# A hybrid decoder trunk on one core: the first product starts with the queries, squares come last, and second halves use a second PSUM pool

## The chip, the core and the metric

The kernel runs on one core of a Trainium2 chip. A core has a matrix engine (TensorE, PE in the rows), a vector engine (VectorE, DVE), a scalar engine for activations and copies (ScalarE, ACT), a general one (GpSimd, POOL), and queues that start transfers from memory; here the queue of SyncE (SP) loads weights, and POOL's queue loads caches and stores results. The metric is the device time of one run in microseconds (us).

## The reference, cut to what matters

Two layers act on 512 prompt tokens and 32 sample tokens (8 sequences of 4), 544 columns in all, of width 1024. Every sub-layer begins with an RMS norm.

```
h = rmsnorm(x, g)                       # x * rsqrt(mean(x*x) + eps) * g
# layer 0: gated linear attention, 4 heads
q, k, v, r, gz = split(h @ w_in)        # 512, 512, 1024, 1024, 16 columns
glog = log_sigmoid(gz @ w_g2 + b_g) / 16
o, state = gla_scan(q, k, v, glog, state)
x = x + (rmsnorm(o, g_norm) * silu(r)) @ w_out
# layer 1: dilated window attention, 3 groups of 16 heads, keys and values of the samples from caches
x = x + combine(groups) @ w_out
# after each layer: convolutional feed-forward, d_ff = 2816
u = h @ w_up
c = causal_conv3(u)
x = x + (silu(gate(c)) * val(c)) @ w_down
```

## The kernel before, in words

Activations lie transposed: the 1024 features are eight tiles (k = 0 to 7) of 128 partitions by 544 tokens. TensorE works on 32-bit numbers that are split in two: `xh` is the rounded high part of x times the norm's gain, `xl` the rest; a weight has `whi` and `wlo`. One product of a 128-column weight block adds `xh*whi`, `xl*whi` and `xh*wlo` over all k. It does so for one half of the tokens and then for the other (two halves of 272, `EVEN`, or 256 and 288, `BYTOK`), so it has 2 x 8 x 3 = 48 matmuls. `product` takes its PSUM tile `ps` from the pool `pm`, which has three buffers. The other pool, `pa`, has five and serves sums of squares (`pss`), gates (`pg`), attention and decoding.

`Normed.add` makes `xh` (ACT) and `xl` (DVE) of an x tile and its square. In the prologue the odd tiles' squares and their sum lie on POOL (`sqp`), the even ones' on ACT and DVE (`sq`, `acc`); elsewhere all squares are ACT's and all sums DVE's. The reciprocal root `rstd` is made when it is first wanted: matmuls with `ones` sum over partitions, ACT takes a logarithm of each half (L181) and an exponential (L124). The norm's factor per token is not in `xh` and `xl`; it is multiplied in where a product is evicted (`scaled`), so an eviction needs `rstd`, the matmuls don't.

The prologue of `gla` loads the gains and the gate weights `wgz`, fills two weight tiles with zeros and puts three copies of the gate weights' high and low parts into them (96 columns each), loads the eight x tiles, and forms the gate product `gz` (48 matmuls), whose eviction needs `rstd`. Then come, for each head, the products q, k and two value products v. For head 0 I call the latter `v0` and `v1`. `gates` and `chain` of a head run as generators between the matmuls of later products (`tick`), and a scheduler then fixes the order on each engine.

In layer 1, four decoding steps j serve the sample tokens, four heads each. `decode_scores` reads keys, `decode_values` the values in seven parts of 1 MB (`vc`, two buffers shared with the keys' `kc`); the matmuls are `pdo`. The out-projection follows; six of its blocks have a last piece, `late`, which adds to x and then feeds the next norm. `ffn` has 22 rounds with two up-products each, evicted with `rstd` into `u` (L566), and down-products that add to x (L196).

Of the kernel before, what the change touches and what calls it, by code (L numbers as in the profile page):

```python
# [11 lines left out]
F32 = mybir.dt.float32  # L12
# [24 lines left out]
def trunk(ctx: ExitStack, tc: tile.TileContext, A, O, stage=4):  # L37
# [58 lines left out]

    def product(w, xh, xl, ranges, done, m=P):

        kt = len(w)
        for n, (a, b) in enumerate(ranges):  # L100
            ps = pm.tile([P, 512], F32, name="ps", tag="ps")
            for k, (hi, lo) in enumerate(w):
                for s, (ww, xx) in enumerate(((hi, xh), (hi, xl), (lo, xh))):
                    mm(ps[:m, :b - a], ww, xx[k][:, a:b],  # L104
                       start=(k == 0 and s == 0), stop=(k == kt - 1 and s == 2))
                if k % 3 == 2 and k < kt - 1:
                    tick()
            done(n, ps[:m, :b - a], slice(a, b))
            tick()


    ident = cp.tile([P, P], F32, name="ident")
    gains = const("gains", [P, 4, KT])
    eps = cp.tile([P, 1], F32, name="eps")
# [5 lines left out]

    last_silu, last_exp = [None], [None]

# [8 lines left out]
    @contextmanager  # L131
    def log_exp():

        with ExitStack() as es:
            if last_silu[0] is not None:
                es.enter_context(tc.issue_after(last_silu[0].ins))
            pre = nc.scalar.preload_act_table_set(LNEXP)
        with tc.issue_after(pre.ins):
            yield
# [4 lines left out]
    class Normed:  # L144
# [3 lines left out]
        def __init__(self, gi):  # L148
            self.gi, self.row, self.acc = gi, None, {}
            self.xh, self.xl = [None] * KT, [None] * KT  # L150

        def add(self, k, x, spare=None):

            g = gains[:, self.gi, k:k + 1]
            h = self.xh[k] = xp.tile([P, NT], F32R, name=f"xh{k}")
            l = self.xl[k] = xp.tile([P, NT], F32R, name=f"xl{k}")
            act(h, x, AF.Copy, scale=g)  # L157
            stt(l, x, g, h.bitcast(F32), ALU.mult, ALU.subtract)  # L158
            i = spare is not None and k % 2
            first = i not in self.acc  # L160
            if i:
                sq = spare.tile([P, NT], F32, name=f"sqp{min(k, 3)}", bufs=2 - first)
                nc.gpsimd.tensor_tensor(out=sq, in0=x, in1=x, op=ALU.mult)
            else:
                sq = xp.tile([P, NT], F32, name="acc" if first else "sq")
                act(sq, x, AF.Square)
            if first:
                self.acc[i] = sq
            else:
                (nc.gpsimd if i else nc.vector).tensor_tensor(out=self.acc[i], in0=self.acc[i], in1=sq, op=ALU.add)  # L170

        @property
        def rstd(self):
            if self.row is None:
                self.row = xp.tile([P, NT], F32, name="rstd")
                with log_exp():
                    for c in (slice(*r) for r in EVEN):
                        ps = pa.tile([P, 512], F32, name="pss", tag="pa")
                        for i, acc in self.acc.items():
                            mm(ps[:, :HN], ones, acc[:, c], start=(i == 0), stop=(i == len(self.acc) - 1))  # L180
                        act(self.row[:, c], ps[:, :HN], AF.Ln, bias=eps, scale=1.0 / 1024)  # L181
                exp(self.row, self.row, scale=-0.5)
            return self.row
# [16 lines left out]
    def gla(nxt):  # L200
# [7 lines left out]

        wz = gconst("wgz", [P, KT, 16])
        whi, wlo = [wp.tile([P, KT, 96], F32R, name=n, tag=n) for n in ("whi", "wlo")]  # L210
        h3, l3 = [t.rearrange("p k (c n) -> p k c n", c=3)[:, :, :, :16] for t in (whi, wlo)]
        wz = wz.unsqueeze(2).to_broadcast([P, KT, 3, 16])
        for t in (whi, wlo):
            nc.vector.tensor_copy(t.rearrange("p k n -> p (k n)"), zero.to_broadcast([P, KT * 96]))
        nc.scalar.copy(h3, wz)
        tt(out=l3, in0=wz, in1=h3.bitcast(F32), op=ALU.subtract)
        nx = Normed(0)
        for k in range(KT):
            x = xtile()
            dma(x, A["xT"][:, k, :])  # L220
            nx.add(k, x, tmp)
        wg2 = gconst("wg2", [96, 512])
        bg = gconst("bg", [P, 4])
        first = load_w(A["wg"][0], KT, 256, "wqk")

        gz = gc.tile([96, NT], F32, name="gz")
        gz3 = gc.tile([96, NT], F32R, name="gz3")
        wg3 = gc.tile([96, 512], F32R, name="wg3")
        product([(whi[:, k], wlo[:, k]) for k in range(KT)], nx.xh, nx.xl, EVEN, scaled(nx, gz, m=96), 96)
        nc.scalar.copy(wg3, wg2)  # L230
# [239 lines left out]
        for h in range(4):  # L470
            G = []
            lanes[1].append(gates(h, G))
            raw = load_w(A["wg"][2 * h], KT, 256, "wqk") if h else first
            q = tmp.tile([P, NT], F32, name="q", bufs=2)
            k = tmp.tile([P, NT], F32, name="k", bufs=2)
            product(split_w(raw, 0, KT, 0), nx.xh, nx.xl, EVEN, scaled(nx, q, P ** -0.5))
            product(split_w(raw, 0, KT, P), nx.xh, nx.xl, EVEN, scaled(nx, k))
            raw = load_w(A["wg"][2 * h + 1], KT, 256, "wv")
            v = [tmp.tile([P, NT], F32, name="vf", bufs=2) for s in range(2)]
            for s in range(2):  # L480
                product(split_w(raw, 0, KT, s * P), nx.xh, nx.xl, EVEN, scaled(nx, v[s]))
            drain()
            lanes[0].append(chain(h, q, k, v, G))
# [8 lines left out]
        for c in range(4):  # L492
            raw = load_w(A["wg"][8 + c], KT, 256, "wr")
            for s in range(2):
# [38 lines left out]
    def ffn(l, x, nx, dst, tables=None, nxt=None):  # L533
        first = load_w(A["wu"][l, 0], KT, 256, "wu")
        with ExitStack() as es:
# [14 lines left out]
            for hf in range(2):  # L550
                gh, gl = [], []
                for ii in range(half):
# [4 lines left out]
                    for s in range(2):  # L557
# [12 lines left out]

                        product(split_w(raw, 0, KT, s * P), nx.xh, nx.xl, BYTOK, done)
                        nc.gpsimd.tensor_copy(  # L572
# [19 lines left out]
                for m in range(KT):  # L592
                    raw = load_w(A["wd"][l, hf, m], half, P, "wd")
                    w = split_w(raw, 0, 6, 0) + split_w(raw, 6, half, 0)
                    product(w, gh, gl, EVEN, added(x[m], x[m]))
                    if hf == 1:
                        (dma if l and m == KT - 1 else dma2)(dst[:, m, :], x[m])
                        if nxt is not None:
                            nxt.add(m, x[m])
# [38 lines left out]
    def dilated(nx, xold, tables, nxt):  # L638
        first = load_w(A["wdi"][0], KT, 256, "wdi")
        with ExitStack() as es:  # L640
# [273 lines left out]
            def decode_scores(j, ks, pace, D):  # L914
# [19 lines left out]
                for part, (cols, width) in enumerate(((((1, 0, 512),), 512), (((0, 0, 128), (2, 128, 384)), 480))):  # L934
# [9 lines left out]
                    for b in range(4):  # L944
# [7 lines left out]
                        if len(kc) < 8:  # L952
                            load()
                    if part:
                        while (2 * j + 1, 1, 0) not in done:
# [9 lines left out]
                done.add(("decode", j))  # L965

            def decode_values(j, vs, pace, D):
                Sd, mx = D["Sd"], D["mx"]
                vc = []

                def load():
                    vc.append(at.tile([P, 4, 512], F32, name="vc", tag="kc"))
                    dma2(vc[-1].rearrange("p a b -> p (a b)"), A["dv"][j, len(vc) - 1])

                load()
                load()
                stt(mx[:, 2:3], mx[:, 0:1], mx[:, 1:2], mx[:, 0:1], ALU.max, ALU.max)
# [29 lines left out]
                for t in range(7):  # L1007
                    for qd in range(4):
                        mm(po[32 * qd:32 * qd + 32, :], PT[:, t, 32 * qd:32 * qd + 32], vc[t][:, qd, :],
                           start=False, stop=(t == 6), skip_group_check=True)  # L1010
                    if t < 5:
                        load()
                    for _ in range(2 * pace if t in (1, 3, 5) else 1 if t == 6 else 0):
                        yield
# [15 lines left out]
            for jj in range(KT):  # L1030
# [59 lines left out]
                if i:  # L1090
                    lanes[1].append(decode_values(j, vs, 9 if j < 3 else 2, D))
                    upto((jj, 1, 0))
# [41 lines left out]
            for m in (6, 0, 1, 2, 3, 4, 5, 7):  # L1134
                if m < 6:
                    product(late[m], ogh[6:], ogl[6:], EVEN, added(x[m], x[m]))
                else:
                    product(split_w(raw, 0, 6, m % 2 * P) + late[m], ogh, ogl, EVEN, old(m))
                nxt.add(m, x[m])
# [76 lines left out]
def layout(inp):  # L1216
# [16 lines left out]
    ch += [w[:, 2048 + 256 * c:2048 + 256 * (c + 1)] for c in range(4)]  # L1233
    d["wg"] = np.stack([chunk(c) for c in ch])
    d["wgz"] = chunk(w[:, 3072:]).reshape(P, KT, 16)
    wg2 = np.zeros((96, 512), np.float32)
    for r in (0, 32, 64):
        wg2[r:r + 16] = a["gla_w_gate2"][0]
# [95 lines left out]
```

## Time and profile before

| | us |
|---|---|
| median of three runs | 1783.75 |
| range | 1783.56 to 1787.02 |
| the profiled execution | 1782.73 |
| its span in the trace | 1781.0 |
| TensorE busy | 1762.5 (99%) |
| DVE, ACT, POOL busy | 1088.0, 802.6, 225.4 |

The span is the stretch of the trace from its first to its last record; the execution's own time is 1.7 us more. A busy TensorE may still run at half of its clock: the granted clock is a column of its own, 1.00 being 2.4 GHz and 0.50 being 1.2 GHz. Times in the trace count from the start of the span. In a timeline the number behind the start is how long the instruction, or the merged run of them, took until its end; matmuls overlap, so their spacing is read from their starts.

### The profile page before, as it was taken

What the parts mean: (1) busy time and instruction counts of PE and PEld (TensorE: products, weight loads), DVE (VectorE), ACT (ScalarE), POOL (GpSimd) and SP (SyncE); (2) the same over time, 40 slices, a digit from 0 to 9 for tenths busy, and PEclk for the clock granted to TensorE, in tenths of its full rate; (3) what the DMA queues carried; (4) which work ended last, traced back from release to release, by engine and by line L of the source; (5) the groups of instructions that cost most, each with busy time, mean ns of one, the idle gap of its engine ahead of it and who ended that gap; (6) DMA issues with size and microseconds to landing.
All of it is one profiled execution on the core that took longest, in us unless ns stands there. A gap on an engine that the chain in (4) does not pass through costs nothing. (4 is left out here: it accounts for less than half of the span.)

```text
span 1781.0 us, 35680 instructions
## 1 busy us (share of the span) xinstructions
PE 1762.5 (99%) x14774; PEld 1672.8 (94%) x14774; DVE 1088.0 (61%) x2552; ACT 802.6 (45%) x1549; POOL 225.4 (13%) x416
## 2 busy tenths in 40 slices
PE   7999999999999999999999999999999999999999
PEld 7999999999999999988998889889888999999999
DVE  7665656764467645666575657666665666347652
ACT  5554544442244435645556465537454434224331
POOL 3000101110011110111012010211121111002100
PEclk9999999999999999999999999999999999999999
DMA  5034432432422244346436643654473222222222
GB/s 183 27 136 152 139 120 74 154 105 82 138 92 95 82 139 180 105 168 220 172 118 208 226 150 129 218 180 151 168 253 139 95 77 75 92 101 96 79 97 87
DMA packets 55266, 236.24 MB, mean 133 GB/s; under 512 B 11470, under 2 KB 20896, under 8 KB 37056
## 3 DMA queue, kind: packets, MB, share of 16 engines
q1 hardware_dynamic: 36816, 145.61, 23.6%
q0 software_dynamic: 18288, 88.36, 13.9%
q8 instruction: 116, 1.90, 0.4%
q14 instruction: 46, 0.38, 0.1%
HBM read 210.32 MB, written 29.33 MB: 135 GB/s over the span
## 5 line engine op out<-in xcount | busy, mean ns | idle before, releaser
L104 PE MATMUL ps<-xh,whi 128*128 128x256 f32 (+2 forms) x3056 | 890.1, 292 | 7.4 <-ACT xh L157 5.4
L104 PE MATMUL ps<-xl,whi 128*128 128x256 f32 (+2 forms) x3056 | 885.8, 290 | 4.0 <-DVE xl L158 4.0
L104 PE MATMUL ps<-xh,wlo 128*128 128x256 f32 (+2 forms) x3056 | 885.4, 290 | 0.7 <-DVE wlo L91 0.7
L104 PEld LDWEIGHTS ps<-xh,whi 128*128 128x128 f32 (+1 forms) x3056 | 576.6, 189 | 25.4 <-issue 15.9
L104 PEld LDWEIGHTS ps<-xl,whi 128*128 128x128 f32 (+1 forms) x3056 | 576.4, 189 | 11.7 <-DVE xl L158 5.6
L104 PEld LDWEIGHTS ps<-xh,wlo 128*128 128x128 f32 (+1 forms) x3056 | 576.2, 189 | 8.9 <-issue 5.9
L104 PE MATMUL ps<-gl,whi 128*128 128x272 f32 x704 | 198.8, 287 | 0.0
L104 PE MATMUL ps<-gh,whi 128*128 128x272 f32 x704 | 198.5, 288 | 0.3 <-DVE x L196 0.3
L104 PE MATMUL ps<-gh,wlo 128*128 128x272 f32 x704 | 195.8, 287 | 0.0
L566 DVE TENSOR_TENSOR u<-ps,rstd 128x256 f32<-128x256 f32 x176 | 74.2, 422 | 141.5 <-PE ps L104 141.1
L90 ACT CAST whi<-wu 128x1024 fp32r<-128x1024 f32 x88 | 92.4, 1050 | 98.1 <-PE ps L104 98.1
L104 PEld LDWEIGHTS ps<-gh,whi 128*128 128x128 f32 x704 | 132.2, 188 | 0.5 <-DVE x L196 0.5
L104 PEld LDWEIGHTS ps<-gl,whi 128*128 128x128 f32 x704 | 132.5, 188 | 0.0
L196 DVE TENSOR_TENSOR x<-ps,x 128x272 f32<-128x272 f32 x108 | 46.7, 439 | 140.5 <-PE ps L104 138.9
L104 PEld LDWEIGHTS ps<-gh,wlo 128*128 128x128 f32 x704 | 130.9, 188 | 0.0
L91 DVE TENSOR_TENSOR wlo<-wu,whi 128x1024 fp32r<-128x1024 f32 x88 | 107.5, 1221 | 32.7 <-ACT whi L90 32.6
L90 ACT CAST whi<-wd 128x768 fp32r<-128x768 f32 x64 | 50.1, 783 | 171.5 <-PE ps L104 142.1
L572 POOL COPY uo<-u 128x18 f32<-128x18 f32 x88 | 53.4, 607 | 401.6 <-DVE u L568 401.6
L91 DVE TENSOR_TENSOR wlo<-wdi,whi 128x1024 fp32r<-128x1024 f32 x72 | 87.9, 1221 | 18.3 <-ACT whi L90 18.2
L90 ACT CAST whi<-wdi 128x1024 fp32r<-128x1024 f32 x72 | 75.2, 1045 | 45.6 <-PE ps L104 36.8
L588 ACT CAST gh<-g 128x544 fp32r<-128x544 f32 x44 | 28.5, 647 | 132.5 <-DVE g L585 132.5
L124 ACT ACTIVATE ex<-ex,nm 128x128 f32<-128x128 f32 (+2 forms) x192 | 74.6, 390 | 25.7 <-DVE nm L748 25.7
(307 smaller groups left out, 2371.9 us busy)
## 6 DMA issues: line engine op xcount, KB each, us to landing
wu<-in_wu SPq DMA_DIRECT2D x44, 1024.0 KB, 4.8
wdi<-in_wdi SPq DMA_DIRECT2D x36, 1024.0 KB, 5.2
vc<-in_dv POOLq DMA_DIRECT2D x28, 1024.0 KB, 7.0
wd<-in_wd SPq DMA_DIRECT2D x32, 704.0 KB, 4.1
kc<-in_dkA POOLq DMA_DIRECT2D x16, 1024.0 KB, 6.5
kc<-in_dkB POOLq DMA_DIRECT2D x16, 768.0 KB, 5.2
out_vo<-v POOLq DMA_DIRECT2D x24, 256.0 KB, 3.0
out_ko<-k POOLq DMA_DIRECT2D x24, 256.0 KB, 2.7
```

The lines of the kernel that those rows point to most:

```text
L90: nc.scalar.copy(hi, r)
L91: tt(out=lo, in0=r, in1=hi.bitcast(F32), op=ALU.subtract)
L104: mm(ps[:m, :b - a], ww, xx[k][:, a:b], start=(k == 0 and s == 0), stop=(k == kt - 1 and s == 2))
L124: last_exp[0] = act(out, in_, AF.Exp, **kw)
L196: tt(out=out[:, c], in0=ps, in1=old[:, c], op=ALU.add)
L566: tt(out=u[:, 2 + c0:258 + c0], in0=ps[:, :256], in1=nx.rstd[:, c0:c0 + 256], op=ALU.mult)
L572: nc.gpsimd.tensor_copy(out=uo[:, f, :].rearrange("p (b t) -> p b t", t=2), in_=u[:, 512:566].rearrange("p (b t) -> p b t", t=6)[:, :, :2])
L588: nc.scalar.copy(h_, g)
```

## The change

It has three parts.

1. Prologue. The gains and gate weights load from ACT's queue. SP's queue loads the q weights of head 0 first (512 KB), then the x tiles, the k weights (512 KB), small tensors and the first value weights. Ten matmuls of `ones` with `ones` are put ahead (`warm`). The gate weights' high and low parts stand side by side in one 96-column tile, so the gate product has 32 matmuls instead of 48. It is formed together with head 0's q product, tile by tile as x comes: ten matmuls for each k. The squares of all x tiles are made afterwards, on ACT, and summed on DVE; POOL makes none. The k product comes next, its first half ahead of the sum of squares; the evictions of q and `gz` wait for `rstd`, ahead of k's. The zero fills are gone.
2. Last decode step. The third value part goes, in four loads of 256 KB, into the tiles `xh6`, `xl6`, `xh7` and `xl7`, which nothing reads any more. The first part is loaded at the end of `decode_scores`, and the parts' matmuls are spread by two ticks each.
3. With `both=True` a product's second half takes its PSUM tile from `pa` instead of `pm`. This holds for the feed-forward's up- and down-products and for the last blocks of the out-projection.

```diff
-    def product(w, xh, xl, ranges, done, m=P):
+    def product(w, xh, xl, ranges, done, m=P, both=False):
...
-            ps = pm.tile([P, 512], F32, name="ps", tag="ps")
+            ps = pa.tile([P, 512], F32, name="ps", tag="pa") if both and n else pm.tile([P, 512], F32, name="ps", tag="ps")
...
+        wz = gc.tile([P, KT, 16], F32, name="wgz")
+        nc.scalar.dma_start(gains, A["gains"])
+        ahead = nc.scalar.dma_start(wz, A["wgz"])
...
+        first = wp.tile([P, 2 * KT, P], F32, name="wqk", tag="wraw")
+        dma(first[:, :KT].rearrange("p k n -> p (k n)"), A["wqk0"][0])
+        warm = pa.tile([P, 512], F32, name="warm", tag="pa")
+        for i in range(10):
+            mm(warm[:, :P], ones, ones, start=True, stop=True)
+
+        wz3 = gc.tile([P, KT, 3, 2, 16], F32R, name="wz3")
...
+        wq = split_w(first, 0, KT, 0)
         nx = Normed(0)
+        xs = [xtile() for k in range(KT)]
         for k in range(KT):
-            x = xtile()
-            dma(x, A["xT"][:, k, :])
-            nx.add(k, x, tmp)
+            dma(xs[k], A["xT"][:, k, :])
+        dma(first[:, KT:].rearrange("p k n -> p (k n)"), A["wqk0"][1])
...
+        for k in range(KT):
+            last = nx.split(k, xs[k])
+            xh, xl, (hi, lo) = nx.xh[k], nx.xl[k], wq[k]
+            for n, (a, b) in enumerate(EVEN):
+                for s, (ps, w, x) in enumerate(((pz, wz3[:, k], xh), (pq, hi, xh), (pq, lo, xh), (pz, wz3[:, k], xl),
+                                                (pq, hi, xl))):
+                    mm(ps[n][:w.shape[1], :HN], w, x[:, a:b], start=(k == 0 and s < 2), stop=(k == KT - 1 and s > 2))
+        with tc.issue_after(last.ins):
+            wk = split_w(first, KT, 2 * KT, 0)
+            for k in range(KT):
+                last = nx.square(xs[k], tmp, 3)
...
+        def earlier(n, ps, c):
+            if n == 0:
+                for n_, c_ in enumerate(slice(*r) for r in EVEN):
+                    scaled(nx, q0, P ** -0.5)(n_, pq[n_][:, :HN], c_)
+                for n_, c_ in enumerate(slice(*r) for r in EVEN):
+                    scaled(nx, gz, m=96)(n_, pz[n_][:96, :HN], c_)
+            scaled(nx, k0)(n, ps, c)
+
+        product(wk, nx.xh, nx.xl, EVEN, earlier)
...
-                        product(split_w(raw, 0, KT, s * P), nx.xh, nx.xl, BYTOK, done)
+                        product(split_w(raw, 0, KT, s * P), nx.xh, nx.xl, BYTOK, done, both=True)
...
-                    product(w, gh, gl, EVEN, added(x[m], x[m]))
+                    product(w, gh, gl, EVEN, added(x[m], x[m]), both=True)
...
+                if j == 3 and len(vc) == 2:
+                    vc.append([xp.tile([P, NT], F32, name="vx", tag=t)[:, :512] for t in ("xh6", "xl6", "xh7", "xl7")])
+                    for qd in range(4):
+                        dma2(vc[-1][qd], src[:, qd * 512:qd * 512 + 512])
...
-                    lanes[1].append(decode_values(j, vs, 9 if j < 3 else 2, D))
+                    lanes[1].append(decode_values(j, vs, 9 if j < 3 else 0, D))
...
-                    product(late[m], ogh[6:], ogl[6:], EVEN, added(x[m], x[m]))
+                    product(late[m], ogh[6:], ogl[6:], EVEN, added(x[m], x[m]), both=True)
                 else:
-                    product(split_w(raw, 0, 6, m % 2 * P) + late[m], ogh, ogl, EVEN, old(m))
+                    product(split_w(raw, 0, 6, m % 2 * P) + late[m], ogh, ogl, EVEN, old(m), both=True)
```

On DVE, in the prologue of before, additions of squares (`acc<-acc,sq`) stand between the low halves `xl` of the x tiles:

```order
L158 SCALAR_TENSOR_TENSOR xl_114<-x,gains,xh_113 128x544 [waits DMAHW4_49,Activation_49]
L170 TENSOR_TENSOR acc<-acc,sq 128x544 [waits Activation_49]
L158 SCALAR_TENSOR_TENSOR xl_123<-x,gains,xh_122 128x544 [waits DMAHW5_49,Activation_49]
L158 SCALAR_TENSOR_TENSOR xl_132<-x,gains,xh_131 128x544 [waits DMAHW6_49,Activation_49]
L158 SCALAR_TENSOR_TENSOR xl_141<-x,gains,xh_140 128x544 [waits DMAHW7_49,Activation_49]
L170 TENSOR_TENSOR acc<-acc,sq 128x544 [waits Activation_49]
L158 SCALAR_TENSOR_TENSOR xl_150<-x,gains,xh_149 128x544 [waits DMAHW0_49,Activation_49]
L158 SCALAR_TENSOR_TENSOR xl_159<-x,gains,xh_158 128x544 [waits DMAHW1_49,Activation_49]
```

In the changed kernel, at the same place, from the last two `xl` on (`wlo<-wqk` is the low half of the k weights, `wg` the second gate weights):

```order
L162 SCALAR_TENSOR_TENSOR xl_222<-x,gains,xh_221 128x544 [waits DMAHW1_49,Activation_49]
L162 SCALAR_TENSOR_TENSOR xl_236<-x,gains,xh_235 128x544 [waits DMAHW2_49,Activation_49]
L172 TENSOR_TENSOR acc<-acc,sq 128x544 [waits Activation_49]
L172 TENSOR_TENSOR acc<-acc,sq 128x544 [waits DVE_49,Activation_49]
L91 TENSOR_TENSOR wlo<-wqk,whi 128x1024 [waits DMAHW3_49,Activation_49]
L172 TENSOR_TENSOR acc<-acc,sq 128x544 [waits DVE_49]
L269 TENSOR_TENSOR wg_280<-wg_127,wg_280 32x512 [waits DMAHW4_49,Activation_49]
L172 TENSOR_TENSOR acc<-acc,sq 128x544 [waits DVE_49,Activation_49] x4
```

All seven additions now follow the last `xl`, with the k weights and the gate weights among them.

On TensorE, the sum of squares `pss` of before stands between the gate product (96 rows) and the q product:

```order
L104 MATMUL ps<-xl_159,whi 96x272
L104 MATMUL ps<-xh_158,wlo 96x272
L180 MATMUL pss<-acc,ones 128x272 [waits DVE_49]
L180 MATMUL pss<-acc,ones 128x272
L104 MATMUL ps<-xh_97,whi 128x272 [waits Activation_49]
L104 MATMUL ps<-xl_98,whi 128x272
L180 MATMUL pss<-sqp_109,ones 128x272 [waits Pool_49]
L180 MATMUL pss<-sqp_109,ones 128x272
```

In the changed kernel it stands between the two halves of the k product:

```order
L105 MATMUL ps<-xh_235,whi 128x272
L105 MATMUL ps<-xl_236,whi 128x272
L105 MATMUL ps<-xh_235,wlo 128x272
L182 MATMUL pss<-acc,ones 128x272 [waits DVE_49]
L182 MATMUL pss<-acc,ones 128x272
L105 MATMUL ps<-xh_137,whi 128x272 [waits DVE_49]
L105 MATMUL ps<-xl_138,whi 128x272
```

The matmul behind it waits for DVE: its buffer is that of q's first half, which is evicted with `rstd`.

On TensorE at the start of the last feed-forward, before, the sum of squares comes when three halves of up-products (256 and 288 columns) are formed or nearly so:

```order
L104 MATMUL ps<-xl_16676,whi 128x288
L104 MATMUL ps<-xh_16675,wlo 128x288
L104 MATMUL ps<-xl_16474,whi 128x256
L104 MATMUL ps<-xh_16473,wlo 128x256
L180 MATMUL pss<-acc,ones 128x272 [waits DVE_49,PE_49]
L180 MATMUL pss<-acc,ones 128x272 [waits PE_49]
L104 MATMUL ps<-xh_16675,whi 128x256
L104 MATMUL ps<-xl_16676,whi 128x256
L104 MATMUL ps<-xh_16675,wlo 128x256
L104 MATMUL ps<-xh_16495,whi 128x288 [waits DVE_49]
```

In the changed kernel it comes when the two first halves are formed, and both second halves (288 columns, in `pa`) follow:

```order
L105 MATMUL ps<-xl_16674,whi 128x256
L105 MATMUL ps<-xh_16673,wlo 128x256
L182 MATMUL pss<-acc,ones 128x272 [waits DVE_49]
L182 MATMUL pss<-acc,ones 128x272
L105 MATMUL ps<-xh_16493,whi 128x288
L105 MATMUL ps<-xl_16494,whi 128x288
L105 MATMUL ps<-xh_16493,wlo 128x288
```

The first matmul behind the sum of squares no longer has a wait for an eviction.

## Rows read from the trace of the kernel before

**Rows 1.** The page, part 1: busy time, share of the span, instructions.
```profile
PE 1762.5 (99%) x14774; PEld 1672.8 (94%) x14774; DVE 1088.0 (61%) x2552; ACT 802.6 (45%) x1549; POOL 225.4 (13%) x416
```

**Rows 2.** Who waited for whom, TensorE, whole span: total us, times, longest.
```profile
PE ps L104 <- ACT xh L157: 5.4, 1, 5.4
PE ps L104 <- DVE xl L158: 4.0, 5, 1.2
PE ps L104 <- DVE u L566: 1.6, 1, 1.6
PE ps L104 <- DVE x L196: 1.5, 3, 0.9
PE pdo L1009 <- DMA vc<-in_dv: 1.0, 2, 0.8
```

**Rows 3.** Timeline of TensorE, prologue: start, duration, instruction, idle before.
```profile
5.44 0.77 PE L104 MATMUL ps<-xh,whi 128*96 128x272 f32 x2 [5.44 <-ACT xh L157]
...
10.23 0.43 PE L104 MATMUL ps<-xh,wlo 128*96 128x272 f32 x1
10.46 0.43 PE L104 MATMUL ps<-xl,whi 128*96 128x272 f32 x1
...
20.89 1.37 PE L180 MATMUL pss<-acc,ones 128*128 128x272 f32 x4
...
29.78 0.41 PE L262 MATMUL pg<-gz,wg 96*128 96x272 f32 x2
...
35.30 0.29 PE L104 MATMUL ps<-xh,whi 128*128 128x272 f32 x1
```

**Rows 4.** Busy time by window: PE, PEld, DVE, ACT, POOL; clock, DMA share, GB/s.
```profile
5.40:11.00 5.60, 4.60 (x19) 4.23 (x20) 5.58 (x4) 4.30 (x7) 4.62 (x4) 1.00 1.04 351
11.00:15.00 4.00, 2.21 (x14) 1.68 (x13) 4.00 (x4) 2.45 (x4) 4.00 (x3) 0.96 1.06 384
15.00:21.00 6.00, 4.79 (x20) 4.04 (x20) 5.94 (x7) 1.69 (x3) 2.10 (x2) 0.50 0.23 96
...
22.00:35.30 13.30, 13.30 (x104) 13.10 (x103) 7.34 (x11) 6.17 (x11) 0.00 (x0) 1.00 0.46 159
```

**Rows 5.** Timeline of DVE, prologue.
```profile
11.06 4.92 DVE L158 SCALAR_TENSOR_TENSOR xl<-x,gains,xh 128x544 fp32r<-128x544 f32 x3
...
17.68 1.47 DVE L158 SCALAR_TENSOR_TENSOR xl<-x,gains,xh 128x544 fp32r<-128x544 f32 x2
...
19.90 0.72 DVE L170 TENSOR_TENSOR acc<-acc,sq 128x544 f32<-128x544 f32 x1
20.54 1.22 DVE L91 TENSOR_TENSOR wlo<-wqk,whi 128x1024 fp32r<-128x1024 f32 x1
...
26.23 0.44 DVE L191 SCALAR_TENSOR_TENSOR q<-ps,rstd 128x272 f32<-128x272 f32 x1 [0.77 <-PE ps L104]
```

**Rows 6.** Timeline of ACT, prologue.
```profile
4.64 0.75 ACT L157 ACTIVATE xh<-x,gains 128x544 fp32r<-128x544 f32 x1 [0.71 <-DMA x<-in_xT]
...
7.69 2.01 ACT L157 ACTIVATE xh<-x,gains 128x544 fp32r<-128x544 f32 x3
...
20.91 1.04 ACT L90 CAST whi<-wqk 128x1024 fp32r<-128x1024 f32 x1 [1.51 <-PE ps L104]
23.01 0.95 ACT L181 ACTIVATE rstd<-pss,eps 128x272 f32<-128x272 f32 x2 [1.06 <-PE pss L180]
23.98 0.66 ACT L124 ACTIVATE rstd<-rstd 128x544 f32<-128x544 f32 x1
```

**Rows 7.** Timeline of SP's queue, prologue.
```profile
1.65 3.75 SPq L47 DMA_DIRECT2D x<-in_xT  x8
```

**Rows 8.** Loads issued from 0 to 36: count, KB each, median us to landing.
```profile
x<-in_xT SPq DMA_DIRECT2D x8, 272.0 KB, 4.4
```

**Rows 9.** Timeline of TensorE, out-projection and start of the last feed-forward.
```profile
1363.14 0.39 PE L104 MATMUL ps<-ogh,late 128*128 128x272 f32 x1 [0.88 <-DVE x L196]
...
1389.00 0.40 PE L104 MATMUL ps<-xh,whi 128*128 128x288 f32 x1 [1.61 <-DVE u L566]
```

## What the change will do to the time

> **What bounds the kernel now.** I read the page first: TensorE is busy for 99% of the span [rows 1], so no faster DVE or ACT helps as such; only TensorE's idle time, its time at half clock and its number of matmuls are to be had. The list of who waited for whom says where the idle time is: 5.4 us before the first matmul, 4.0 us in five waits for low halves `xl`, and later 1.6 us for an `u` eviction, 1.5 us in three waits for an `x` update, 1.0 us in two waits for parts of the decode values [rows 2]. Those five rows make 13.5 us, and the change aims at each.
>
> The timeline shows the prologue. The gate product begins at 5.44, the sum of squares at 20.89, and the first value product (`v0`, the first work that does the same thing at the same place in both kernels) at 35.30 [rows 3]. So 15.45 us pass under 48 gate matmuls, which at full rate would need about 6. Two things stretch them. First the rate: two neighbours at 10.23 and 10.46 stand 0.23 us apart [rows 3], while from 22 on 104 matmuls fill 13.30 us, 0.128 each [rows 4]; the windows give the granted clock as 0.50 from 15 to 21 and 1.00 from 22 on [rows 4], that is 1.2 and 2.4 GHz. Second the feed: three `xl` take 4.92 us on DVE, 1.64 each, and the last two 1.47, 0.73 each [rows 5]. The slow ones lie in the stretch in which POOL is busy for 4.00 of 4 us, and the fast ones after it [rows 4]. Squares on POOL thus more than double the price of what TensorE waits for.
>
> **The prologue after the change.** I rebuild it up to the start of `v0`.
>
> *Loads.* The queue issues the eight x tiles from 1.65 to 5.40 [rows 7], the last at about 4.9. Issue to landing takes a median 4.4 us [rows 8]; the first took 3.0, since its ACT work begins at 4.64 [rows 6], so the last may take 5.8. That is 9.3 to 10.7 for the last x; I take 10.5. Now 512 KB of q weights go ahead of x, 1.5 us at the 351 GB/s of that stretch [rows 4], and the two small loads leave the queue, 0.9 us earlier. Last x: 11.1. The first issue moves up to about 0.75 (1.65 less 0.9), and 512 KB need 0.7 more than a tile's 272 KB: the q weights are there at 0.75 + 3.0 + 0.7 = 4.4.
>
> *First matmul.* The cast of the q weights' high half takes 1.04, an `xh` 0.67 [rows 6]: 4.4 + 1.04 + 0.67 is 6.1, 0.7 later than now. The ten warm matmuls end before that and lie in idle time; they cost nothing.
>
> *The joint product.* Gate and q together are 80 matmuls instead of 48 + 48. At 0.128 they need 10.2 us, with about 1 us of early waits for the first low halves: until 17.3. `xl` without POOL costs 0.73, and the last ends at 11.1 + 0.67 + 0.73 = 12.5. The feed is no longer what holds TensorE. The first half of the k product, 24 matmuls or 3.1 us, needs no normalisation and takes the third buffer: until 20.4.
>
> *The sum of squares.* It comes last now, serially. DVE has seven adds of 0.72, the low half of the k weights, 1.22, and a short low half of the gate weights, which I bound by an `xl`, 0.73 [rows 5]: 7.0 us. A square costs ACT about what an `xh` does, 0.67. DVE starts at 12.5, waits 0.6 for the second square and 1.0 for the cast of the k weights, which stands behind four squares on ACT. Sum: 12.5 + 7.0 + 1.6 = 21.1. Four passes over `ones` at about 0.13, two logarithms (0.95) and an exponential (0.66) [rows 6] make the reciprocal root ready at 23.2. q's first half is then evicted, 0.44 [rows 5], which frees its buffer, and the second half of k begins at 23.6 and ends 24 x 0.128 = 3.1 later. `v0`: 26.7. Between 20.4 and 23.6 TensorE has only the four passes: this is the new stall, about 2.7 us, on the path.
>
> *Balance.* Before, 35.30, less 0.25 for the two `pg` matmuls [rows 3] that now come after the start of `v0`: 35.05. At full clock the gain is 8.4. But matmuls right after the start ran at half rate for five us and more [rows 3]. If the same happens here, some 20 of the 80 cost 0.1 more, the first half of k ends at 22 and not 20.4, later than the squares, and `v0` is at 27.7: gain 7.3. I take this. Then the stall: from 11 to 15 TensorE was busy for 2.21 of 4 us, and from 15 to 21 its clock was 0.50 [rows 4]. A stall of over 2 us may do that again; the 24 matmuls behind it cost between nothing and 24 x 0.1 = 2.4 more. I take 1.0. **Prologue: 6.3, between 2 and 8.4.**
>
> The Trainium skill (TensorE: Matmul & The Clock Gate, "HAM oscillation — how this bites in real kernels") says that a TensorE that waits between batches of matmuls falls back to half clock and starts the next batch cold; it speaks against putting all squares last. By that rule the 2.4 is lost whole and the prologue gives 4.9. The windows from 11 to 21 agree with it as far as they go [rows 4].
>
> What else the change takes out of the prologue (two zero fills on DVE, four of the eight passes over `ones`) lay under waits for loads or is already left out of the chain above. What it puts on ACT's queue, two small loads ahead of the table load, ends before the first weights land.
>
> **The last decode step.** Its two waits are 1.0 in sum [rows 2]. A value part can be loaded only when one of two buffers is free; with the third part in x's dead tiles, each later part is loaded one place earlier in the chain, by more than the two waits need. The parts are the same bytes on the same queue. What stands behind the four new loads on POOL's queue are reloads of `x` and the value outputs; neither is waited for in [rows 2]. Gain 0 to 1.0; I take 0.9.
>
> **Both pools.** Out-projection: idle 0.88 before 1363.14 [rows 9], with three buffers waiting for `x` updates on DVE behind a weight split; second halves in the other pool give it up to five more evictions' time. Gain 0.8. FFN of layer 1: 1.61 before 1389.00 [rows 9]; three buffers were full until the reciprocal root existed. Now the sum of squares stands ahead of the long second halves, which fill 2 x 24 x 0.13 = 6 us, more than the 2.2 that the root needs: 1.6 gone. The other two of the three `x` waits are 1.5 - 0.9 = 0.6 [rows 2]; the decode step's new spread leaves more products ahead of the out-projection: 0.4. Sum 2.8. **Late: 0.9 + 2.8 = 3.7, between 1 and 4.1.** Elsewhere the engines' order is that of before or nearly so, and the sum has no term; I allow 1 us either way.
>
> **The rivals.**
> *Forecast, 0.38:* 6.3 + 3.7 = 10.0 us off the profiled 1782.73: 1772.7. The runs' median is 1.0 above the profiled one, so runs may show 1773.7; I say 1773.
> *Cold after the stall, 0.17:* the stall takes the clock to half, and all 24 matmuls of k's second half run at it: 7.3 - 2.4 + 3.7 = 8.6, 1774.1. For it: the windows from 11 to 21. Against: from 15 on, TensorE's waits came one after another, and here it is a single one. This is the time by the rule of the Trainium skill (TensorE: Matmul & The Clock Gate, the section named above).
> *Full clock, 0.12:* the warm matmuls do their work and the stall costs no clock: 8.4 + 4 = 12.4, 1770.3. Against it: before, five us of matmuls were not enough [rows 3].
> *Cold prologue, 0.18:* half clock for about 40 matmuls more than I count (the first 20 and the 24 after the stall, and some of `v0`): 6.3 - 0.1 x 40 = 2.3, total 6, 1776.7. The half-clock stretch before the sum of squares speaks for it.
> *The late parts don't do what they say, 0.11:* decode parts share the DMA engines with the out-projection's weights and land as late as now, and the freed buffers run into the same DVE queue: late 0.5 to 1, total 7, 1775.7.
> *Slower, 0.04:* TensorE stays at half clock through `v0` and `v1`. In the prologue alone (80 + 48 matmuls at 0.227) `v0` begins at 6.1 + 1 + 29 + 2 = 38, 3 later than now, and 96 more matmuls lose 9.6: -12.6 + 3.7, or 1791.6. It becomes a loss once some 100 matmuls beyond my 30 are cold. Against it: from 15 to 21 TensorE was busy 4.79 of 6 us, and from 22 the clock was 1.00 [rows 4]; the joint product keeps it as busy.
>
> **How the numbers follow.** The forecast's own range is 1770 to 1775.5. The first five cases, with the bounds of their terms and the 1.0 between profile and median, reach from 1769 to about 1779, which leaves out no more than 2 in 10. A measurement here tells 0.2%, 3.6 us, from no change: all cases but the last are faster by more, and the tails of the cold prologue and of the late parts reach into no change: faster 0.91, same 0.06, slower 0.03.
>
> **What would show it.** Right: first joint matmul at 5.5 to 6.5; `xl` at about 0.75; sum of squares at 20 to 22.5; one wait of 1 to 3 us for q's eviction; `v0` at 27 to 30; none of the waits for `u`, and less than 1 us in sum for `x` and the value parts. Wrong: `xl` still near 1.6, so POOL wasn't the cause; x landing after 13; a clock of 0.5 past `v0`; or new idle time in the FFNs, where the sum has none.

## The result, and the profile after

| | before | changed |
|---|---|---|
| median of 6 runs, us | 1783.76 | 1772.42 |
| range, us | 1783.37 to 1787.02 | 1770.22 to 1776.95 |
| the profiled execution, us | 1782.73 | 1773.47 |
| span in the trace, us | 1781.0 | 1771.6 |
| TensorE busy, us | 1762.5 | 1760.5 |

The changed kernel takes 0.9934 of the time before (95% interval 0.9918 to 0.9950). That is 11.3 us between medians and 9.3 between the profiled executions; I forecast 10.0 between profiled executions and 1773 as time. The sum held, but not all of its terms, as the profile shows. Its runs also spread over 6.7 us, and the experiments show what most of that goes with.

Who waited for whom on TensorE, whole span of the changed kernel; it answers to [rows 2]:

```profile
PE pdo L1061 <- DMA vc<-in_dv: 2.3, 1, 2.3
PE ps L105 <- DVE q L193: 1.7, 1, 1.7
PE warm L221 <- DVE ones L120: 1.1, 1, 1.1
PE ps L245 <- ACT xh L161: 1.0, 1, 1.0
PE ps L105 <- DVE wlo L91: 0.5, 1, 0.5
PE ps L105 <- DVE xl L162: 0.3, 1, 0.3
PE ps L245 <- DVE xl L162: 0.2, 1, 0.2
```

The waits for `xl`, for `u` and for `x` are gone or nearly so. The first row of [rows 2], 5.4 us before the first matmul, is gone in this list alone: the warm matmuls fill that time, and the first matmul on data begins at 6.33, against 5.44 before. The stall that I expected, q's eviction, is there with 1.7 us. But the first row shown here is against the forecast: the wait for a part of the decode values has grown from 1.0 to 2.3.

The timeline of TensorE in the changed prologue, answering to [rows 3]:

```profile
1.12 4.23 PE L221 MATMUL warm<-ones 128*128 128x128 f32 x20 [1.12 <-DVE ones L120]
6.33 0.52 PE L245 MATMUL ps<-xh,whi 128*128 128x272 f32 x2 [0.98 <-ACT xh L161]
...
10.30 0.43 PE L245 MATMUL ps<-xl,whi 128*128 128x272 f32 x1
10.52 0.43 PE L245 MATMUL pz<-xl,wz 128*96 128x272 f32 x1
...
21.83 1.08 PE L182 MATMUL pss<-acc,ones 128*128 128x272 f32 x4
24.65 0.39 PE L105 MATMUL ps<-xh,whi 128*128 128x272 f32 x1 [1.74 <-DVE q L193]
...
27.75 0.28 PE L105 MATMUL ps<-xh,whi 128*128 128x272 f32 x1
```

The joint product begins at 6.33, the sum of squares at 21.83, k's second half at 24.65, and `v0` at 27.75, against 35.30 before. Busy time and clock by window (columns as in [rows 4]):

```profile
6.10:11.00 4.90, 4.41 (x21) 3.97 (x22) 4.90 (x8) 4.90 (x9) 0.00 (x0) 0.71 1.03 392
11.00:15.00 4.00, 4.00 (x31) 4.00 (x31) 3.80 (x6) 4.00 (x8) 0.00 (x0) 0.92 1.03 367
15.00:21.00 6.00, 6.00 (x50) 6.00 (x49) 5.62 (x8) 3.44 (x5) 0.00 (x0) 1.00 0.80 269
21.00:27.00 6.00, 4.26 (x30) 3.75 (x30) 2.92 (x7) 2.25 (x4) 0.00 (x0) 1.00 0.32 113
```

The clock is at its lower level for part of the time up to 12, as I assumed, and stays at 1.00 through the stall and behind it. In the kernel before, two waits lay between 11 and 15, ahead of the stretch at 0.50:

```profile
12.72 0.37 PE L104 MATMUL ps<-xl,whi 128*96 128x272 f32 x1 [1.24 <-DVE xl L158]
...
14.26 0.37 PE L104 MATMUL ps<-xl,whi 128*96 128x272 f32 x1 [0.55 <-DVE xl L158]
```

On DVE and ACT of the changed kernel:

```profile
7.96 4.95 DVE L162 SCALAR_TENSOR_TENSOR xl<-x,gains,xh 128x544 fp32r<-128x544 f32 x7
12.83 1.55 DVE L172 TENSOR_TENSOR acc<-acc,sq 128x544 f32<-128x544 f32 x2
...
17.08 3.22 DVE L172 TENSOR_TENSOR acc<-acc,sq 128x544 f32<-128x544 f32 x4
```

```profile
22.49 0.95 ACT L183 ACTIVATE rstd<-pss,eps 128x272 f32<-128x272 f32 x2 [2.44 <-PE pss L182]
23.46 0.66 ACT L125 ACTIVATE rstd<-rstd 128x544 f32<-128x544 f32 x1
```

Seven low halves take 4.95 us, 0.71 each, where three took 4.92 [rows 5]; the last ends at 12.9. The sums end at about 20.3, so what fixed the sum of squares at 21.83 was TensorE, still busy with k's first half.

Where the rest moved is read by setting the same instructions of both traces against each other. The lead over before was 7.3 us at the first `px` of head 0, 9.4 at the start of layer 0's out-projection, 10.4 to 10.5 through the first three decoding steps, 9.2 at the end of the fourth, 10.0 at the first down-product of the last feed-forward, and 9.4 at the end. So the prologue gave 7.3, layer 0's attention 2 more, and the stretch up to the decoding steps 1.0; the last decode step took 1.3 back, the out-projection with the start of the feed-forward gave 0.8, and the last 270 us took 0.6 back. Three smaller waits of before, which [rows 2] leaves out, have no counterpart at their places:

```profile
PE ps L104 <- DVE wlo L91: 0.7, 1, 0.7
PE ptr L892 <- DVE ex L873: 0.4, 1, 0.4
PE po L907 <- DVE PT L896: 0.3, 1, 0.3
```

The first lies in head 1 of layer 0's attention, the other two just ahead of the first decoding step.

Which piece of the prologue gave how much of the 7.3, no run splits in full. Twenty matmuls fewer (16 of the gate product, four of the sums) are some 2.6 us at 0.128 each, which is an estimate; `e7_pool_squares` below prices the squares on POOL; the order of the sums alone has no run.

### The profile page after: what moved, and what is told of

Same layout as the page of the kernel before. It is cut to its first block, busy times and chain, and to the rows that moved or that the text cites. A ratio compares the mean times of both kernels' runs of the same rounds, so it can differ in the third digit from the quotient of the medians.

```text
span 1771.6 us, 35608 instructions
## 1 busy us (share of the span) xinstructions
PE 1760.5 (99%) x14774; PEld 1671.7 (94%) x14774; DVE 1082.1 (61%) x2554; ACT 804.4 (45%) x1553; POOL 216.3 (12%) x412
## 4 chain that ended last, share of the span: by engine, by line
PE 97%; DMA 1%; DVE 1%; issue 0%; ACT 0%; POOL 0%; POOLq 0%; DVEq 0%
PE ps L105 82%; PE po L948 2%; PE pd L990 2%; PE pdo L1061 2%; DMA vc<-in_dv 1%; PE ptr L933 1%; PE pn L735 1%; PE pn L736 1%; PE pvt L803 1%; PE psc L842 1%; PE psc L837 0%; PE psc L839 0%; PE pu L440 0%; PE px L428 0%; PE po L455 0%; PE ps L245 0%
## 5 line engine op out<-in xcount | busy, mean ns | idle before, releaser
L105 PE MATMUL ps<-xh,whi 128*128 128x256 f32 (+2 forms) x3024 | 879.0, 291 | 1.7 <-DVE q L193 1.7
L105 PE MATMUL ps<-xl,whi 128*128 128x256 f32 (+2 forms) x3024 | 872.5, 289 | 0.3 <-DVE xl L162 0.3
L105 PEld LDWEIGHTS ps<-xh,whi 128*128 128x128 f32 x3024 | 570.5, 189 | 17.6 <-issue 14.5
L105 PEld LDWEIGHTS ps<-xh,wlo 128*128 128x128 f32 x3024 | 568.1, 188 | 12.3 <-issue 9.6
L105 PEld LDWEIGHTS ps<-xl,whi 128*128 128x128 f32 x3024 | 569.6, 188 | 7.0 <-issue 4.8
```

Source lines behind the costliest of these rows:

```text
L105: mm(ps[:m, :b - a], ww, xx[k][:, a:b], start=(k == 0 and s == 0), stop=(k == kt - 1 and s == 2))
```

## The experiments

Times are medians; "before" means the kernel before, run beside them on the same chip.

**One part alone, and one part left out.** `e2_pools` is the kernel before with the `both=True` edits alone, `e3_decode` with the new last decode step alone. `e4_no_decode` is the changed kernel with the old decode step:

```diff
-                        elif j == 3:
-                            values_part(j, D)
...
-                for _ in range(2 if pace else 1):
-                    values_part(j, D)
...
+                load()
+                load()
...
-                    lanes[1].append(decode_values(j, vs, 9 if j < 3 else 0, D))
+                    lanes[1].append(decode_values(j, vs, 9 if j < 3 else 2, D))
```

`e1_prologue` has this edit and one more, which leaves the new prologue alone:

```diff
-            ps = pa.tile([P, 512], F32, name="ps", tag="pa") if both and n else pm.tile([P, 512], F32, name="ps", tag="ps")
+            ps = pa.tile([P, 512], F32, name="ps", tag="pa") if False else pm.tile([P, 512], F32, name="ps", tag="ps")
```

> The kernel before with the new prologue alone. Theory: the change's gain is mostly the prologue's; the traces of before and after put the first value product at 35.30 and 27.75, and the same place in head 2's chain 9.0 us apart, so this kernel should be 8.5 to 9.5 us faster than before, about 1774.7. Rival: the prologue's start is earlier but the time is given back in the attention of layer 0; then 5 to 7 us.

> The kernel before with second halves in the other PSUM pool alone. Theory: it removes the waits of 1.6 us for the eviction of u, 0.88 and 0.29 us for x updates: 2.3 to 2.8 us faster, about 1781.2. Rival: the buffers only let the products run into the next weight split, and the gain is under 1 us.

> The kernel before with the change of the last decode step alone. Theory from the trace of after (one wait of 2.3 us for a value part, against two of 1.0 us in sum): it is a loss of 0.5 to 1.5 us. Rival, my prediction's term: a gain of 0.9 us.

> The changed kernel with the last decode step as before. Theory: the decode part costs about 1.3 us where it waits and gives back about 0.4 us ahead of the out-projection, so this kernel is about 1 us faster than the changed one, near 1771.5, with waits for value parts of 1.0 us. Rival: the decode part helps by 0.9 us, and this kernel is at 1773.3 or more.

| | median, us | runs | to before (95%) |
|---|---|---|---|
| e1_prologue | 1773.88 | 5 | 0.9944 (0.9931 to 0.9956) |
| e2_pools | 1781.18 | 11 | 0.9987 (0.9978 to 0.9996) |
| e3_decode | 1783.11 | 11 | 0.9993 (0.9984 to 1.0002) |
| e4_no_decode | 1772.08 | 5 | 0.9936 (0.9922 to 0.9949) |
| before | 1784.35 | 21 | |

The prologue alone is 10.5 us by medians (7.8 to 12.3 by the interval) and 9.5 between the profiled spans; the theory's 8.5 to 9.5 lies within the interval. The rival, that layer 0 gives some back, falls: the lead grows there, to 9.1 at the out-projection. The pools alone give 3.2 (0.7 to 3.9). In their trace the waits for `u` and `x` are gone, and two smaller ones have come at the start of the last feed-forward, 0.5 for `wlo` and 0.4 for `xl`. The stretch from the last `pdo` matmul to the first down-product of the last feed-forward is 161.6 us in it, against 163.2 before: 1.6. The decode step can't be told from no change by these runs. In its profile the value parts waited 0.4 us, without it (`e4_no_decode`) 1.2, in the changed kernel 2.3, and in `e2_pools`, whose decode step is the old one, 2.4. So this wait differs from execution to execution by more than the decode part could give. In the profile of `e3_decode` the waits for `x` are down to 0.3 as well, the same waits that the pools take away, so the two parts don't simply add. And where both are present, the stretch named above is 162.4 us in all eight profiles; with the pools and the old decode step it is 161.6 to 161.7 in three (`e2_pools`, `e4_no_decode`, `e12_late_wu_old_decode`). The new decode step thus costs 0.7 us there, whatever it gives ahead of it. My theory for `e3_decode`, a loss of 0.5 to 1.5, rested on one profile and isn't borne out; `e4_no_decode`, expected at 1771.5, is 0.3 us faster than the changed kernel, well inside the spread.

**What makes the value parts late.** `e10_late_wu` keeps the changed kernel but issues three loads of the last feed-forward, 1.4 MB, behind the last value part:

```diff
-        first = load_w(A["wu"][l, 0], KT, 256, "wu")
+        if l:
+            first = wp.tile([P, KT, 256], F32, name="wu", tag="wraw")
+            with tc.issue_after(last_vc[0].ins):
+                dma2(first.rearrange("p k n -> p (k n)"), A["wu"][l, 0])
+        else:
+            first = load_w(A["wu"][l, 0], KT, 256, "wu")
...
-            dma(cw, A["cw"][l])
+            (dma2 if l else dma)(cw, A["cw"][l])
...
-            dma(cs, A["cs"][l])
+            (dma2 if l else dma)(cs, A["cs"][l])
```

> The changed kernel with three loads of the last feed-forward (up-weights, convolution weights and states) issued behind the last value part, on its queue. Theory: the sixth value part took 10.1 us to land since these 1.4 MB shared the transfer engines with it; without them it lands in 6 to 8 us and the wait of 2.27 us before 1334.29 falls under 0.6: 1.5 to 2.3 us faster than after. Rival: the value parts are late for the buffers' sake, being issued when the products free them; the wait stays over 1.5 us.

It ran at 1770.58 (4 runs, 1770.32 to 1771.34; 0.9923 of before, 0.9910 to 0.9936). `e14_late_wu_again` is the same kernel, run beside a second run of the changed kernel, `after_again`.

> The kernel with late loads once more, beside the other three. Theory: no wait for a value part over 0.3 us, median 1770 to 1771.5, all runs within 2 us. Rival: the narrow spread of its first four runs was luck; a range of 4 us or more.

> The changed kernel once more, unchanged. Theory: its runs differ among each other since the sixth value part lands at different times (and the clock's start by some tenths); so this run's profile has one wait for a value part of 1 to 3 us, its first value product between 26.7 and 28.1, and its times lie between 1770 and 1777 with a median 1 to 3 us above the kernel with late loads. Rival: the spread comes from the clock, and the profile shows half-clock stretches past 12.

`e14_late_wu_again`: 1770.77, 5 runs from 1769.73 to 1771.34. `after_again`: 1772.69, 6 runs from 1771.29 to 1777.82. The sixth value part's load alone, in the changed kernel and then in `e14_late_wu_again` (its issue, who waited for it, and its time to landing):

```profile
L1020 POOL DMA_DIRECT2D vc<-in_dv x1: 530/530/530, 1324.2 to 1324.2; - x1
...
  PE pdo L1061: 2.3, 1
...
DMA to landing us min/median/max: 10.1/10.1/10.1
```

```profile
L1025 POOL DMA_DIRECT2D vc<-in_dv x1: 530/530/530, 1324.3 to 1324.3; - x1
...
DMA to landing us min/median/max: 5.0/5.0/5.0
```

Issued 0.1 us apart, the part lands after 10.1 us in the one and 5.0 in the other, and in the second TensorE doesn't wait for it. In `after_again` it took 8.9 and TensorE waited 1.1. The rival, that buffers make the parts late, falls for this part. With the loads out of the way nine runs lie within 1.6 us, while twelve of the changed kernel spread over 7.6 (one of them, 1777.82, lies above the 1777 that I expected at most): most of its spread goes with these early loads. What TensorE waited in its slowest runs wasn't recorded, since only one run of each kernel is profiled.

`e12_late_wu_old_decode` has the late loads and the old decode step (the edits of `e4_no_decode` and `e10_late_wu` together).

> The changed kernel with the late loads of the feed-forward but the last decode step as before. Theory: with the contention gone the old decode step still waits at its last parts for their buffers, 0.3 to 1 us, so it is 0.3 to 1.2 us slower than the kernel with late loads and the new decode step. Rival: once the loads are late the decode change is worth nothing, and the two agree within 0.3 us.

It ran at 1769.78, 5 runs from 1769.20 to 1770.49 (0.9924 of before, 0.9912 to 0.9935): 1.0 us faster than `e14_late_wu_again` beside it. Neither theory said that. In its profile one part is waited for, 0.6 us, but the stretch from the end of the fourth step to the down-products takes 0.7 us less than in `e14_late_wu_again`. So the two about cancel by the traces, and the 1.0 between medians, of five runs each whose ranges overlap, isn't clear of noise. On top of the other two parts the decode part is worth nothing or slightly less, with early loads and with late ones. This version is the fastest of the study: 13.7 us below before by medians, 2.9 below the changed kernel beside it.

**The prologue's pieces.** `e7_pool_squares` makes four of the squares on POOL while x is split:

```diff
             last = nx.split(k, xs[k])
+            if k % 2:
+                sqp[k] = tmp.tile([P, NT], F32, name="sqp", tag="rt", bufs=5)
+                nc.gpsimd.tensor_tensor(out=sqp[k], in0=xs[k], in1=xs[k], op=ALU.mult)
```

> The changed kernel with the squares of the four odd x tiles made on POOL while x is split; the sums stay on DVE. Theory: a low half that runs beside a POOL square takes 1.4 to 1.7 us instead of 0.71, the last one ends 2 to 4 us later, and although ACT has four squares less the sum of squares is 0.5 to 2.5 us later than at 21.83. Rival: POOL was not what made the low halves slow in the kernel before; they stay near 0.71 and the sum of squares comes no later.

It ran at 1777.59 (0.9967 of before, 0.9954 to 0.9980), 5.2 us above the changed kernel's median. Its DVE, and its POOL:

```profile
6.90 1.61 DVE L162 SCALAR_TENSOR_TENSOR xl<-x,gains,xh 128x544 fp32r<-128x544 f32 x1
8.44 1.45 DVE L226 TENSOR_TENSOR wz<-wgz,wz 128x384 fp32r<-128x384 f32 x1
9.80 6.62 DVE L162 SCALAR_TENSOR_TENSOR xl<-x,gains,xh 128x544 fp32r<-128x544 f32 x7
```

```profile
6.67 1.26 POOL L244 TENSOR_TENSOR sqp<-x 128x544 f32<-128x544 f32 x1 [3.21 <-DMA x<-in_xT]
8.12 4.24 POOL L244 TENSOR_TENSOR sqp<-x 128x544 f32<-128x544 f32 x3 [0.19 <-DMA x<-in_xT]
```

The first `xl` and the gate weights' low half, which lie beside the first POOL squares, take 1.61 and 1.45 us instead of 0.78 and 0.55; the last `xl` ends at 16.4 instead of 12.9, and the sum of squares starts at 24.74, 2.9 later than at 21.83 (the expectation's upper bound was 2.5). The theory holds: POOL's squares slow the low halves, and four of them cost 2.9 us up to the sum of squares. The other 2.3 us between the medians aren't accounted for; the spread of kernels with early loads is larger than that.

`e5_no_warm` is the changed kernel without the ten warm matmuls, `e13_late_wu_no_warm` the same with late loads.

```diff
-        warm = pa.tile([P, 512], F32, name="warm", tag="pa")
-        for i in range(10):
-            mm(warm[:, :P], ones, ones, start=True, stop=True)
```

> The changed kernel without the ten warm matmuls. Theory: in the trace of after the clock was full from the first joint matmul at 6.33 to about 8.2, then half until 11.4; the warm matmuls bought that full stretch and no more. Without them the matmuls before 8.2 (11 of them, spaced by waits anyway) run at half: at most 1 us later, and nothing at all at the sum of squares when the squares end last: 0 to 1 us slower than after. Rival: without them the clock rises later than 11.4, and the first half of k ends at 23 or later: 1.5 to 3 us slower.

> The kernel with late loads, without the warm matmuls. Theory: with the noise of the value parts gone the warm matmuls show as what the two traces gave them, v0 at 28.15 against 27.5: 0.3 to 1.0 us slower than with them. Rival: they were worth the 2.5 us that the medians of the kernels with early loads differed by.

`e5_no_warm`: 1774.93 (0.9946, 0.9934 to 0.9958), 2.5 above the changed kernel, but its profile has 2.8 us of waiting for a value part, and `v0` at 28.15. `e13_late_wu_no_warm`: 1771.08, 5 runs from 1770.09 to 1771.50, 0.3 us above `e14_late_wu_again`; `v0` stands at 27.76 and 27.79 in the two profiles. In the other six profiles with this prologue unaltered it stands between 26.78 (`e4_no_decode`) and 28.07 (`e1_prologue`). In `after_again`, with `v0` at 26.85, 30 matmuls were made from 6 to 11; in `e13_late_wu_no_warm` 18. Of the eight profiles that have the warm matmuls and this start, three made 30 to 32 matmuls from 6 to 11 (`after_again`, `e4_no_decode`, `e6_k_pool`) and five 18 to 21, as both profiles without them did. So in some executions the clock is up early and about 1 us is gained, in the others nothing; that the warm matmuls do this is likely, but two profiles without them don't show it. In the median they are worth 0.3, which is not clear of noise. Most of the 2.5 us of `e5_no_warm` is then likely to be the value parts.

**Taking the new stall away.** `e6_k_pool` puts the second half of head 0's k product into the other pool, so that it need not wait for q's eviction:

```diff
-        product(wk, nx.xh, nx.xl, EVEN, earlier)
+        product(wk, nx.xh, nx.xl, EVEN, earlier, both=True)
```

> The changed kernel with the second half of head 0's k product in the other pool, so that it needs no eviction of q. Theory: the wait of 1.74 us before 24.65 is gone, because 24 matmuls (3.0 us) cover the 2.8 us of logarithm, exponential and eviction: 1.5 to 2.1 us faster than after. Rival: the next product, v0, waits for a buffer in its turn, and the gain is under 0.5 us.

It ran at 1785.23 (12 runs, 1781.43 to 1791.25; 1.0009 of before, 0.9998 to 1.0019): some 13 us slower than the changed kernel. The stall is gone, and `v0` starts at 24.90, 2.85 earlier than in the changed kernel. About 0.9 of this goes with the clock, up early in this execution: the sum of squares begins at 20.89 here and not at 21.83; from there to `v0` it is 4.0 us against 5.9, so the stall gave 1.9. All of it and 12.7 us more are lost in layer 0. The waits on TensorE in its attention, from 28 to 230, and two of them in the timeline:

```profile
PE ps L105 <- ACT whi L90: 7.7, 4, 4.0
PE pot L467 <- ACT on L570: 0.6, 1, 0.6
PE pu L440 <- DVE S L443: 0.2, 1, 0.2
```

```profile
98.56 0.60 PE L105 MATMUL ps<-xh,whi 128*128 128x272 f32 x1 [2.92 <-ACT whi L90]
...
182.99 0.40 PE L105 MATMUL ps<-xh,whi 128*128 128x272 f32 x1 [3.98 <-ACT whi L90]
```

ACT's cast before them waited for the weights' load, and SP's queue for stores of states. SP's waits from 60 to 200, in `e6_k_pool` and then in the changed kernel:

```profile
SPq L47 <- DMA out_sgs<-S: 127.9, 6, 45.9
```

```profile
SPq L47 <- DMA out_sgs<-S: 110.3, 6, 40.0
```

The weights of a later head stand on SP's queue behind loads of that head's states, and those wait until the states of an earlier head are stored. In `e6_k_pool` the weight loads of the third stretch are issued at 131.24 and not at 122.76: the scheduler has put the heads' own work later among the products, so states are stored later, while the products come sooner. (The first `px` of head 0 starts at 48.32 here and at 48.40 there, so for the heads' own work the 2.85 us are gone by then.) Of the 15.6 us lost, 7.7 are these waits; the rest lies in TensorE's clock, 0.91 from 100 to 130 and 0.96 from 160 to 200 against 1.00 in the changed kernel, and in single matmuls waiting one for the other, which I haven't split further. Neither expectation had this.

## Why the prediction was right, and where it wasn't

- **Which rows bound the kernel:** right for three of the five rows of [rows 2], `xl`, `u` and `x`. The first gave nothing, since work on data starts 0.9 us later than before, as the sum's 6.1 for the first matmul had it; the fifth grew.
- **First matmul at 6.1, last `xl` at 12.5, k's first half until 22:** measured 6.33, 12.9, 21.83. The price of `xl` without POOL, 0.73, measured 0.71, and `e7_pool_squares` shows the cause.
- **Sum of squares ready at 21.1:** the sums ended at 20.3; the 1.6 us of waits for ACT that I charged didn't occur, DVE worked from 12.8 to 20.3 without one. It didn't matter here, since TensorE came last, as the half-clock case said. In `after_again` and `e4_no_decode`, whose first half came sooner, TensorE did wait for the sums, 0.3 and 0.5 us.
- **The stall:** 1.74 us where I had 2.7 with an idle TensorE; behind a first half that ends at 22, as in the forecast's case, the same numbers give about 2. Right in place and releaser. (With my 20 slow matmuls at 0.1 more each, 20.4 would have become 22.4 and not 22; 21.83 was measured.)
- **The clock behind the stall, 1.0 us:** wrong. The 24 matmuls from 24.7 to 27.7 ran at full clock, and no profile of this prologue shows otherwise from 15 on. From 11 to 15 of before TensorE was idle for 1.79 of 4 us, in the two waits shown above, and its clock fell to 0.50; here it was idle for 1.74 in one, behind ten us without a gap, and it didn't. The rule of the Trainium skill (TensorE: Matmul & The Clock Gate, "HAM oscillation — how this bites in real kernels"), that a TensorE waiting between batches starts the next one cold, is told there of a kernel with longer waits, for loads; this stall of 1.74 us didn't bring it about. One reading of [rows 4] needs care: it gives 1.00 from 5.40 to 11.00, although the gate matmuls stand 0.23 us apart there [rows 3], as they do later at 0.50. The forecast went by the spacing, rightly.
- **Prologue 6.3:** measured 7.3, that is the 7.3 I had before the clock term. Other executions put `v0` from 26.78 to 28.07, and those with the old prologue from 34.83 (`e3_decode`) to 36.47 (`e2_pools`), so the gain lies between 6.5 and 9.4.
- **Layer 0's attention, no term, 1 us allowed:** wrong by size: 2.0, in `e1_prologue` too. A wait of 0.7 for a low half of weights in head 1 is gone; the rest I haven't traced. The stretch up to the decoding steps, also without a term, gave 1.0 more, of which 0.7 are the two waits ahead of the first step.
- **Last decode step, 0.9:** wrong in its mechanism. "Each later part is loaded one place earlier" is true by order, but the last parts' landing is set by other loads on the same transfer engines: that is my rival of the late parts, for this part, with the feed-forward's loads in place of the out-projection's weights. `e3_decode`, `e4_no_decode` and `e12_late_wu_old_decode` show no effect clear of noise. My own sign of being right, less than 1 us in sum for `x` and the value parts, failed: the value parts alone took 2.3.
- **Both pools, 2.8:** the waits I named are gone, and `e2_pools` measures 0.7 to 3.9. By the traces the pools brought less: 1.6 with the old decode step, 0.8 with the new one. In the changed kernel two new waits, 0.5 and 0.3, take back part of it.
- **The sum:** 10.0 against 9.3 by profile and 11.3 by median. That it is so near is luck. In the profiled execution all up to the decoding steps gave 10.4 where the sum had 6.3, and all from there on took 1.1 back where the sum had 3.7: an underestimate of 4 us stood against an overestimate of nearly 5. What holds is the main mechanism, a prologue fed faster with the stall where I put it; the late parts don't.

## What to carry to other kernels

- Where TensorE waits for the low half of a split, look at what runs on POOL beside DVE: four squares put back on POOL cost 2.9 us here. What the order of the sums alone is worth, no run shows.
- A transfer that was issued one place earlier was of no use here while another queue's loads were under way beside it; find the loads that aren't yet needed and issue them behind it. That took 2 us and most of the spread between runs away.
- Before removing a stall in a scheduled kernel, ask what its order downstream is tuned to: taking a stall of 1.74 us out of the prologue cost some 15 us later, about half of it by weight loads behind loads that wait for a store.

## What the runs showed of the hardware that I hadn't expected

A 1 MB transfer issued at the same moment landed in 5.0 us or in 10.1, depending on 1.4 MB issued by another queue within 2 us. And a single pause of 1.74 us, after ten us of gapless matmuls, left the clock at its higher level, where two gaps of nearly the same sum within 4 us had been followed by the lower one.
